# First-layer feed-forward: two of three token chunks of gate and up by one Strassen level

## The chip, the cores and the metric

One core of one Trainium2 chip. The metric is device time in microseconds (us) of one execution; a lower one is better. Engines: PE (matmuls) with its weight loads PEld, DVE (vector), ACT (scalar), POOL (GpSimd), and SP, which issues the loads from memory.

## What is computed

A decoder trunk of two layers on 1024 tokens plus 16 meta tokens, width 1024, everything float32. Each layer adds a token mixer (layer 0: pooling, layer 1: differential attention) and then a SwiGLU feed-forward with 2816 features. The change touches the feed-forward of layer 0:

```
h = h + swiglu(rms_norm(h, ffn_norm_g[i]), ffn_w_gate[i], ffn_w_up[i], ffn_w_down[i])

def swiglu(h, w_gate, w_up, w_down):
    return (jax.nn.silu(h @ w_gate) * (h @ w_up)) @ w_down
```

## The kernel before

Activations lie with the width on the partitions, as 8 tiles (k) of 128 rows. The 1040 tokens are three chunks of 348, 348 and 344 columns (`WC`). The 2816 features are 22 tiles of 128, taken in 11 pairs. Each float32 factor is split into a high part (rounded to the matmul's format by an ACT copy) and a low part (the rest, by a subtraction, mostly on DVE); `mm3` (lines 166 to 172) multiplies high x high, high x low and low x high into one PSUM bank, so that one 128 x 128 tile of a product is three matmuls.

The feed-forward of layer 0 is `ffn` (line 539). For a feature and a chunk, `phase_a` runs gate and up over 8 k-tiles into the two banks of one `psA` tile (two such tiles), then ACT takes Silu (line 556), DVE multiplies (558), ACT and DVE split the activation (561, 562). For a pair of features and a chunk, `phase_b` computes the 8 row tiles of the down product into `psB` banks (four) and DVE adds each to h (574). Gate and up weights go through a raw tile (two buffers), and high and low tiles `wh` and `wl` (four each) in `wp`; down weights are split into the eight `keep` slots `d0` to `d7`. The order inside the first pair (with mixer and norms woven in) and the last pair (with the norm of the next layer) is written out; pairs 1 to 9 (lines 618 to 625) are plain loops. `weave`, `drain` and `fill` advance several generators in turn, which gives the instructions their order; a planner that simulates a timeline then puts each engine's instructions in order by that priority, and starts what is ready when the first choice waits. All loads of weights are issued by SP, in one queue.

Layer 1's feed-forward (`wino`, line 1202, `twist_gen`, line 1128) already uses one Strassen level (Winograd's form) for its two halves of 512 tokens: a pair of features by two halves of the width is a 2 x 2 block matrix A, two halves of the width by two token halves a 2 x 2 matrix B, and seven products of half the width take the place of eight. POOL forms the sums of A's blocks (1225), `unit` splits each block (1110, 1111), the sums of B are formed once (`twist_gen`, tiles T1 to T3; T4 takes the place of a part of the input). Products 1, 6 and 5 add up in one bank X, 7 and 4 in one bank W of tile `xw`; `hold` copies a bank to SBUF by ACT (1213), `put` adds X to it by DVE (1217). So product 6 may add into X only when the put of block (0,0) has read it, product 5 only when the put of (1,0) has.

Of the kernel before, what the change touches and what calls it, by code (L numbers as in the profile page):

```python
# [8 lines left out]
F32 = mybir.dt.float32  # L9
# [90 lines left out]
class Trunk:  # L100
# [34 lines left out]
    def slot(self, i, dt, nm):  # L135
        return self.keep.tile([P, L], dt, tag=f"d{i}", name=nm)

# [149 lines left out]
    def band_setup(self, mx, raw):  # L287
        nc = self.nc
        zero = mx.tile([P, ZPAD], F32, name="zero")
        self.bt = mx.tile([P, ZPAD + 4 * (BANDW + ZPAD)], F32R, name="bt")  # L290
# [248 lines left out]
    def ffn(self, l, xn, rng, done, head=None, hook=None, tailhook=None, nf=2, pre=None, begin=None, cs=range(NCH)):  # L539
# [43 lines left out]
        def load_d(f, eng=None):  # L583
            down[f] = self.load_w(ap["down"][l * FT + f], self.keep, f"d{l}_{f}", "d", eng)

        for j, fs in enumerate(chunks):
            first, last = j == 0, j == len(chunks) - 1
            if first or last:
                if first and pre:
                    ws = {}  # L590
                else:
                    ws = {f: load_gu(f) for f in fs}
                    for f in fs:
                        load_d(f)
            if first:
# [158 lines left out]
    def scores(self, h, s, i):  # L754
# [37 lines left out]
        bias = s["bias"][:, BW - bw :]  # L792
        negm = self.sp.tile([P, 2], F32, tag="negm", name=f"negm_{h}_{i}")
        ssum = self.sp.tile([P, 2], F32, tag="ssum", name=f"ssum_{h}_{i}")
        E = []
        rs = self.sp.tile([P, 2], F32, tag="rs", name=f"rs_{h}_{i}")
        E = [None, None]
# [836 lines left out]
```

## Time and profile before

| | us |
|---|---|
| median of 3 runs | 2161.59 (2161.29 to 2165.12) |
| profiled execution | 2161.81 |
| its span, first to last instruction | 2160.0 |
| PE busy | 2101.2 (97%) |
| DVE, ACT, POOL busy | 1249.1, 809.7, 506.0 |

Busy time is the union of the intervals in which an engine had an instruction running. Matmuls overlap each other in this record, so their mean duration is longer than the time that one adds; the distance between starts is what one costs in a full stream. The granted clock is PE's, as a share of 2.4 GHz (0.50 is 1.2 GHz). The feed-forward of layer 0 runs from about 76 to 840 us, attention to about 1390, the rest is layer 1's end.

### The profile page before, as it was taken

The page shows a single profiled execution, that of the slowest core. Times are in us where ns is not written, and L with a number is a line of the kernel's source. Part 1 is how long each engine was busy: PE and PEld are TensorE (multiplying, and loading weights), DVE is VectorE, ACT ScalarE, POOL GpSimd, SP SyncE. Part 2 cuts the span into 40 slices and gives each one's busy share as a digit, 9 for nine tenths or more (in the row PEclk, how much of TensorE's full clock was granted, in tenths as well). Part 3 has the DMA queues.
Part 4 walks back from the last instruction along what each step waited for, and adds up shares of the span by engine and source line. Part 5 has one row for each costly group of instructions (what it writes and reads, how often), then busy time and mean ns, then how long its engine had stood idle before and what let it go on. Part 6 is the DMA issues. An engine that isn't in the chain of part 4 may idle for free.

```text
span 2160.0 us, 30440 instructions
## 1 busy us (share of the span) xinstructions
PE 2101.2 (97%) x12150; PEld 1952.2 (90%) x12150; DVE 1249.1 (58%) x2109; ACT 809.7 (37%) x1664; POOL 506.0 (23%) x628
## 2 busy tenths in 40 slices
PE   7999999999999999999999999998899999999997
PEld 7999999999999999999999998876788888888886
DVE  6653333433333337667667767569766666666655
ACT  5531211112111215666666665443333333333224
POOL 4300000000000015444444334137421122222113
PEclk8999999999999999999999999999999999999998
DMA  7021111111101102122111135421111111111102
GB/s 242 27 62 59 56 33 40 49 59 42 47 30 59 59 27 92 54 62 62 52 42 62 50 129 188 152 71 40 41 58 59 59 39 59 59 46 52 59 20 78
DMA packets 52696, 139.27 MB, mean 64 GB/s; under 512 B 5618, under 2 KB 17435, under 8 KB 52555
## 3 DMA queue, kind: packets, MB, share of 16 engines
q1 hardware_dynamic: 52555, 137.34, 19.5%
q8 instruction: 95, 1.56, 0.3%
q14 instruction: 46, 0.38, 0.1%
HBM read 115.16 MB, written 17.90 MB: 62 GB/s over the span
## 4 chain that ended last, share of the span: by engine, by line
PE 89%; DVE 6%; ACT 3%; DMA 1%; issue 1%; POOL 0%; SPq 0%; DVEq 0%; ACTq 0%; POOLq 0%
PE gu L171 9%; PE gu L170 8%; PE gu L172 8%; PE pj L172 4%; PE pj L170 4%; PE pj L171 4%; PE y L170 4%; PE y L171 4%; PE y L172 4%; PE yd L170 3%; PE yd L171 3%; PE yd L172 3%; PE o L860 2%; PE xw_u L170 2%; PE xw_u L172 2%; PE xw_g L171 2%
## 5 line engine op out<-in xcount | busy, mean ns | idle before, releaser
L574 DVE TENSOR_TENSOR h<-h,y 128x348 f32<-128x348 f32 (+1 forms) x264 | 134.4, 514 | 158.3 <-PE y L172 158.1
L170 PE MATMUL pj<-xh_m,w_h 128*128 128x348 f32 (+2 forms) x576 | 187.9, 326 | 0.6 <-DVE oo L896 0.6
L172 PE MATMUL pj<-xh_m,w_l 128*128 128x348 f32 (+2 forms) x576 | 185.4, 322 | 0.0
L556 ACT ACTIVATE s<-gu 128x348 f32<-128x348 f32 (+1 forms) x66 | 30.2, 458 | 412.2 <-PE gu L172 412.0
L171 PE MATMUL pj<-xl_m,w_h 128*128 128x348 f32 (+2 forms) x576 | 184.1, 320 | 0.0
L1301 DVE TENSOR_TENSOR H<-H,yd 128x512 f32<-128x512 f32 (+1 forms) x184 | 120.2, 662 | 89.1 <-PE yd L172 88.0
L199 POOL TENSOR_TENSOR acc_m<-sq_m,sq_m 128x348 f32<-128x348 f32 (+1 forms) x3 | 2.8, 929 | 673.6 <-ACT sq_m L188 673.6
L170 PE MATMUL y<-ah,d_h 128*128 128x348 f32 (+1 forms) x480 | 155.1, 324 | 3.0 <-DVE h L574 2.9
L170 PE MATMUL yd<-ah,d 128*128 128x512 f32 (+1 forms) x368 | 142.7, 392 | 12.9 <-DVE H L1301 7.8
L171 PE MATMUL y<-al,d_h 128*128 128x348 f32 (+1 forms) x480 | 154.7, 322 | 0.0
L172 PE MATMUL y<-ah,d_l 128*128 128x348 f32 (+1 forms) x480 | 154.4, 322 | 0.0
L170 PE MATMUL gu<-xh_f,g_h 128*128 128x348 f32 (+1 forms) x480 | 153.9, 321 | 0.0
L170 PE MATMUL gu<-xh_f,u_h 128*128 128x348 f32 (+1 forms) x480 | 153.9, 321 | 0.0
L171 PE MATMUL gu<-xl_f,g_h 128*128 128x348 f32 (+1 forms) x480 | 153.8, 320 | 0.0
L171 PE MATMUL gu<-xl_f,u_h 128*128 128x348 f32 (+1 forms) x480 | 153.8, 320 | 0.0
L172 PE MATMUL gu<-xh_f,g_l 128*128 128x348 f32 (+1 forms) x480 | 153.6, 320 | 0.0
L172 PE MATMUL gu<-xh_f,u_l 128*128 128x348 f32 (+1 forms) x480 | 153.5, 320 | 0.0
L171 PE MATMUL yd<-al,d 128*128 128x512 f32 (+1 forms) x368 | 142.4, 387 | 0.5 <-DVE al L1111 0.5
L172 PE MATMUL yd<-ah,d 128*128 128x512 f32 (+1 forms) x368 | 140.8, 386 | 0.0
L558 DVE TENSOR_TENSOR s<-gu,s 128x348 f32<-128x348 f32 (+1 forms) x66 | 34.1, 516 | 171.9 <-ACT s L556 171.9
L170 PEld LDWEIGHTS pj<-xh_m,w_h 128*128 128x128 f32 x576 | 108.5, 188 | 1.4 <-DVE oo L896 0.9
L171 PEld LDWEIGHTS pj<-xl_m,w_h 128*128 128x128 f32 x576 | 108.6, 188 | 0.5
(438 smaller groups left out, 5885.1 us busy)
## 6 DMA issues: line engine op xcount, KB each, us to landing
raw_d<-in_down_dram SPq DMA_DIRECT2D x42, 512.0 KB, 4.5
raw_g<-in_gate_dram SPq DMA_DIRECT2D x38, 512.0 KB, 4.5
raw_u<-in_up_dram SPq DMA_DIRECT2D x38, 512.0 KB, 4.5
raw_w<-in_wqkv_dram SPq DMA_DIRECT2D x24, 512.0 KB, 3.3
odram<-oo SPq DMA_DIRECT2D x28, 256.0 KB, 2.4
ox<-odram SPq DMA_DIRECT2D x4, 1536.0 KB, 7.1
qk<-qk SPq DMA_DIRECT2D x16, 260.0 KB, 2.9
raw_woe<-in_wo_dram SPq DMA_DIRECT2D x8, 512.0 KB, 3.6
```

Source lines behind the costliest of these rows:

```text
L170: nc.tensor.matmul(out, wh, xh, start=first, stop=False, skip_group_check=skip)
L171: nc.tensor.matmul(out, wh, xl, start=False, stop=False, skip_group_check=skip)
L172: nc.tensor.matmul(out, wl, xh, start=False, stop=last, skip_group_check=skip)
L199: eng.tensor_tensor(acc[:, :w], x[:, :w], sq[:, :w], op=ALU.add)
L556: nc.scalar.activation(st[:, :w], ps[:, 0, :w], AF.Silu)
L558: nc.vector.tensor_tensor(at[:, :w], ps[:, 1, :w], st[:, :w], op=ALU.mult)
L574: nc.vector.tensor_tensor(h[:, m, a:b], h[:, m, a:b], ps[:, :w], op=ALU.add)
L860: nc.tensor.matmul(po[:, : 2 * P], ah[:rows, kb, :], s["vhl"][:rows, kb, :], start=j == 0, stop=j == nl)
L1301: self.nc.vector.tensor_tensor(h, h, ps, op=ALU.add)
```

## The change

In layer 0, pairs 2 to 9 (eight pairs) compute gate and up of chunks 0 and 1 with the seven products; the third chunk runs beside them with the same split weight pieces as plain products (V0, V1). A side is gate or up of one pair: eight weight pieces of 512 columns (seven products, and one for the third chunk), in a ring of six tiles made of the four `wl` and the two `raw` buffers (`ring0`). The raw rows go to the four `wh` buffers (`raw0`); POOL forms the sums of blocks in place. Temporary rows come from 13 existing tiles (`t0`). The tiles T1 to T3 take all eight `keep` slots, so down weights of these pairs are split into the same ring (`down0`), and the down product of a pair is run between gate and up of the next. Pair 1 is plain, in chunk order 1, 0, 2, and the rows T are formed beside it (`twist0`, all on DVE); its down product comes with pair 2. At the end T4's part of the input is restored beside the down product of pair 9, and then the last pair loads its down weights as before. The slots grow from 1040 to 1044 columns; a zero tile of the start and three statistics tiles of attention are placed elsewhere.

```diff
         for j, fs in enumerate(chunks):
             first, last = j == 0, j == len(chunks) - 1
-            if first or last:
+            if first or last or j == 1:
                 if first and pre:
                     ws = {}
                 else:
                     ws = {f: load_gu(f) for f in fs}
-                    for f in fs:
-                        load_d(f)
...
+            elif j == 1:
+                self.nd = 0
+                tw = self.twist0(xn)
+                run = seq(*[phase_a(f, c, *ws[f]) for c in (1, 0, 2) for f in fs])
+                while not next(tw):
+                    fill(run, 3)
+                while not next(tw):
+                    fill(run, 2)
+                drain(run)
             elif last:
+                drain(self.down0(j - 1, acts), tw)
+                for f in fs:
+                    load_d(f)
...
-                for f in fs:
-                    ws = load_gu(f)
-                    load_d(f)
-                    for c in cs:
-                        drain(phase_a(f, c, *ws))
-                for c in cs:
-                    drain(phase_b(j, fs, c))
+                sg = {}
+                drain(self.gate0(j, xn, sg))
+                drain(self.down0(j - 1, acts))
+                drain(self.up0(j, xn, sg, acts))
+
+    def ring0(self, nm):
+        self.nring = getattr(self, "nring", -1) + 1
+        tag = ("wl", "raw", "wl")[self.nring % 3]
...
+    def twist0(self, xn):
...
+        for k in range(4):
+            b11, b12, b22 = part(0, 0, k), part(1, 0, k), part(1, 1, k)
+            t3 = diff(f"u3_{k}", b22, b12)
+            self.split(t3, *pair(3, k))
+            yield
+            t2 = more(f"u2_{k}", b11, t3, ALU.add)
+            self.split(t2, *pair(2, k))
+            yield
+            t1 = diff(f"u1_{k}", b12, b11)
+            self.split(t1, *pair(1, k))
+            yield
+        yield True
+        for k in range(4):
+            t4 = diff(f"u4_{k}", part(0, 1, k), [t.bitcast(F32) for t in pair(2, k)])
+            self.split(t4, *pair(4, k))
+            yield
...
+    def wino0(self, p, nm, src, xn, use):
...
+        V1 = bank("v1")[:, :w2]
+        mul(8, A[2, 1], (V1, bx(0, 2), True, False, False))
+        yield
+        V0 = bank("v0")[:, :w2]
+        mul(1, A[1, 1], (X, bx(0, 0), True, True, False), (V0, bx(0, 2), True, False, False))
+        G.tensor_tensor(A[1, 1], A[1, 1], A[2, 1], op=ALU.subtract)
+        G.tensor_tensor(A[2, 1], A[2, 1], A[2, 2], op=ALU.add)
+        yield
+        Y = bank("y0")[:, :WMAX]
+        mul(2, A[1, 2], (Y, bx(1, 0), True, True, False), (V0, bx(1, 2), False, True, False))
+        hold(0, 0, Y)
+        put(0, 0, X)
+        use(0, 2, V0)
+        yield
+        mul(7, A[1, 1], (W, bt(3), True, True, False))
+        hold(1, 1, W)
+        G.tensor_tensor(A[1, 1], A[2, 2], A[1, 1], op=ALU.subtract)
+        G.tensor_tensor(A[1, 2], A[1, 2], A[1, 1], op=ALU.subtract)
+        yield
+        mul(6, A[1, 1], (X, bt(2), False, True, True))
+        yield
+        mul(4, A[2, 2], (W, bt(4), False, True, True), (V1, bx(1, 2), False, True, False))
+        hold(1, 0, W)
+        put(1, 0, X)
+        use(1, 2, V1)
+        yield
+        Z = bank("z0")[:, :WMAX]
+        mul(3, A[1, 2], (Z, bx(1, 1), True, True, False))
+        hold(0, 1, Z)
+        yield
+        mul(5, A[2, 1], (X, bt(1), False, True, True))
+        put(0, 1, X)
+        put(1, 1, X)
+        yield
...
+    def down0(self, p, acts):
+        nc = self.nc
+        raw = [self.raw0(self.ap["down"][2 * p + i], f"raw_d0_{p}_{i}") for i in range(2)]
+        a = {(i, c): acts.pop((2 * p + i, c)) for i in range(2) for c in range(NCH)}
+        for q in range(2):
+            u = [self.unit0(raw[i][:, q * HALF : q * HALF + HALF], f"d0_{p}_{q}{i}") for i in range(2)]
+            for e in range(4):
+                m = 4 * q + e
+                for c in range(NCH):
+                    ps = self.psb(f"y0_{p}_{m}_{c}")[:, : WC[c]]
+                    for i in range(2):
+                        ww = [t[:, e * P : e * P + P] for t in u[i]]
+                        self.mm3(ps, ww, a[i, c], i == 0, i == 1)
+                    h = self.hs[c][:, m, : WC[c]]
+                    nc.vector.tensor_tensor(h, h, ps, op=ALU.add)
+                yield
```

## Rows read from the trace of the kernel before

**Rows 1.** The page: busy time of each engine with its share of the span and its instructions, PE's granted clock in 40 slices (tenths), and the chain that ended last by engine.

```profile
PE 2101.2 (97%) x12150; PEld 1952.2 (90%) x12150; DVE 1249.1 (58%) x2109; ACT 809.7 (37%) x1664; POOL 506.0 (23%) x628
...
PEclk8999999999999999999999999999999999999998
...
PE 89%; DVE 6%; ACT 3%; DMA 1%; issue 1%; POOL 0%; SPq 0%; DVEq 0%; ACTq 0%; POOLq 0%
```

**Rows 2.** Busy time by stretches of 100 us in the feed-forward of layer 0: stretch, its length, busy us and instructions of PE, PEld, DVE, ACT and POOL, granted clock, share of the load engines, GB/s.

```profile
200.00:300.00 100.00, 100.00 (x634) 100.00 (x634) 36.54 (x65) 12.58 (x20) 0.00 (x0) 1.00 0.12 38
300.00:400.00 100.00, 100.00 (x635) 100.00 (x634) 33.94 (x54) 20.34 (x31) 0.00 (x0) 1.00 0.17 52
400.00:500.00 100.00, 100.00 (x634) 100.00 (x633) 41.12 (x72) 14.58 (x24) 0.00 (x0) 1.00 0.14 44
```

**Rows 3.** Instructions of PE in order of time, first and last of 37 starts in a row (start us, us, engine, line, operation).

```profile
208.40 0.32 PE L170 MATMUL y<-ah,d_h 128*128 128x348 f32 x1
...
214.08 0.32 PE L170 MATMUL y<-ah,d_h 128*128 128x344 f32 x1
```

**Rows 4.** The page's groups of instructions: one line of `mm3` in the down product and in gate, over the ten pairs 1 to 10 (count, busy us, mean ns of one).

```profile
L170 PE MATMUL y<-ah,d_h 128*128 128x348 f32 (+1 forms) x480 | 155.1, 324 | 3.0 <-DVE h L574 2.9
...
L170 PE MATMUL gu<-xh_f,g_h 128*128 128x348 f32 (+1 forms) x480 | 153.9, 321 | 0.0
```

**Rows 5.** The same table of stretches as rows 2, in layer 1's feed-forward with its seven products.

```profile
1600.00:1700.00 100.00, 100.00 (x443) 82.84 (x442) 65.42 (x83) 34.92 (x61) 24.31 (x15) 1.00 0.16 53
1700.00:1800.00 100.00, 100.00 (x443) 82.84 (x442) 62.50 (x83) 30.25 (x52) 18.77 (x12) 1.00 0.16 53
1800.00:1900.00 100.00, 100.00 (x442) 82.80 (x442) 66.24 (x86) 34.08 (x59) 20.48 (x13) 1.00 0.16 53
```

**Rows 6.** Groups in the stretch 1600 to 2000 us, engine by engine: low halves of weight pieces of 512 columns (from a sum, z; of down), of activations, put; ACT's copies of a piece and of a bank; POOL's sums.

```profile
L1111 DVE TENSOR_TENSOR al<-cu,ah 128x512 fp32r<-128x512 f32 x28 | 41.5, 1482 | 1.0
L1111 DVE TENSOR_TENSOR d<-raw_d,d 128x512 fp32r<-128x512 f32 x27 | 29.9, 1128 | 0.0
...
L1111 DVE TENSOR_TENSOR w_g<-z,w_g 128x512 fp32r<-128x512 f32 x28 | 19.3, 689 | 23.0 <-ACT w_g L1110 23.0
...
L1217 DVE TENSOR_TENSOR cu<-cu,xw_u 128x512 f32<-128x512 f32 x28 | 18.6, 686 | 32.1 <-ACT cu L1213 27.1 <-PE xw_u L172 5.0
...
L1110 ACT CAST w_g<-z 128x512 fp32r<-128x512 f32 x28 | 17.4, 622 | 30.9 <-PE xw_u L172 19.3 <-issue 11.6
...
L1225 POOL TENSOR_TENSOR z<-raw_u 128x512 f32<-128x512 f32 x14 | 22.5, 1626 | 101.1 <-DMA raw_u<-in_up_dram 101.1
```

**Rows 7.** Groups in the stretch 160 to 800 us, each shape by itself: DVE's add to h, low half of 1024 columns, low half and multiply of 348; ACT's copy and Silu of 348.

```profile
L574 DVE TENSOR_TENSOR h<-h,y 128x348 f32<-128x348 f32 x149 | 76.0, 515 | 99.5 <-PE y L172 99.5
...
L160 DVE TENSOR_TENSOR g_l<-raw_g,g_h 128x1024 fp32r<-128x1024 f32 x18 | 22.1, 1225 | 46.2 <-ACT g_h L156 46.2
...
L562 DVE TENSOR_TENSOR al<-s,ah 128x348 fp32r<-128x348 f32 x39 | 20.3, 521 | 21.0 <-ACT ah L561 20.9
L558 DVE TENSOR_TENSOR s<-gu,s 128x348 f32<-128x348 f32 x39 | 20.3, 521 | 168.3 <-ACT s L556 168.3
...
L561 ACT CAST ah<-s 128x348 fp32r<-128x348 f32 x39 | 18.8, 483 | 22.9 <-DVE s L558 22.9
L556 ACT ACTIVATE s<-gu 128x348 f32<-128x348 f32 x39 | 18.0, 461 | 405.1 <-PE gu L172 405.1
```

**Rows 8.** Instructions in order of time around one hand-over of bank X in layer 1: the last matmul of product 4, another product's first, ACT's hold, DVE's put and what follows it, the first matmul of product 5.

```profile
1622.79 0.39 PE L172 MATMUL xw_u<-x_f,w_u 128*128 128x512 f32 x1
1623.02 0.39 PE L170 MATMUL y_g<-x_f,w_g 128*128 128x512 f32 x1
1623.22 0.58 ACT L1213 COPY cu<-xw_u 128x512 f32<-128x512 f32 x1 [2.04 <-PE xw_u L172]
...
1623.83 0.69 DVE L1217 TENSOR_TENSOR cu<-cu,xw_u 128x512 f32<-128x512 f32 x1 [1.94 <-ACT cu L1213]
...
1624.56 0.69 DVE L1283 TENSOR_TENSOR cu<-cu,cg 128x512 f32<-128x512 f32 x1
...
1625.74 0.39 PE L170 MATMUL xw_u<-T,w_u 128*128 128x512 f32 x1
```

**Rows 9.** Instructions in order of time: a low half of 512 columns on DVE beside a sum on POOL.

```profile
1673.20 1.62 POOL L1225 TENSOR_TENSOR z<-z,raw_g 128x512 f32<-128x512 f32 x1
1673.60 1.77 DVE L1111 TENSOR_TENSOR al<-cu,ah 128x512 fp32r<-128x512 f32 x1
```

**Rows 10.** Groups of PE in the stretch 120 to 154.8 us (to the end of pair 0's down product): the first and the last of the six groups of pair 1's gate and up (five of 8, one of 7).

```profile
L172 PE MATMUL gu<-xh_f,g_l 128*128 128x348 f32 x8 | 2.6, 322 | 0.0
...
L172 PE MATMUL gu<-xh_f,u_l 128*128 128x348 f32 x7 | 2.2, 320 | 0.0
```

**Rows 11.** The table of stretches in layer 1 while its rows T are formed.

```profile
1480.00:1500.00 20.00, 14.73 (x53) 10.71 (x51) 19.96 (x19) 5.43 (x11) 16.84 (x11) 0.83 0.15 52
1500.00:1520.00 20.00, 12.54 (x46) 9.60 (x47) 20.00 (x22) 4.01 (x7) 15.26 (x10) 0.91 0.00 1
1520.00:1540.00 20.00, 16.21 (x63) 12.64 (x62) 18.16 (x20) 7.22 (x13) 12.56 (x8) 0.91 0.16 53
```

**Rows 12.** The page's list of loads: count, KB each, median us from issue to landing.

```profile
raw_g<-in_gate_dram SPq DMA_DIRECT2D x38, 512.0 KB, 4.5
```

More of the change, by code (lines that the diff above doesn't have):

```diff
@@ L135, in slot @@
     def slot(self, i, dt, nm):
-        return self.keep.tile([P, L], dt, tag=f"d{i}", name=nm)
+        return self.keep.tile([P, 3 * WMAX], dt, tag=f"d{i}", name=nm)
     def small(self, dt, nm):
@@ L288, in band_setup @@
         nc = self.nc
-        zero = mx.tile([P, ZPAD], F32, name="zero")
+        zero = self.tp.tile([P, WMAX], F32, tag="xt", bufs=3, name="zero")[:, :ZPAD]
         self.bt = mx.tile([P, ZPAD + 4 * (BANDW + ZPAD)], F32R, name="bt")
@@ new lines, in wino0, with hold, put, bank @@
+    def wino0(self, p, nm, src, xn, use):
+        nc, ap = self.nc, self.ap
+        V, G = nc.vector, nc.gpsimd
+        held = {}
+        def hold(i, j, b):
+            t = held[i, j] = self.t0(f"c{nm}0_{p}_{i}{j}")
+            nc.scalar.copy(t, b)
+        def put(i, j, b):
+            t = held.pop((i, j))
+            V.tensor_tensor(t, t, b, op=ALU.add)
+            use(i, j, t)
+        raw = [self.raw0(ap[src][2 * p + i], f"raw_{nm}0_{p}_{i}") for i in range(2)]
+        A = {(i + 1, k + 1): raw[i][:, k * HALF : k * HALF + HALF] for i in range(2) for k in range(2)}
+        w2 = WC[2]
+        xw = self.psa(f"xw_{nm}0_{p}")
+        X, W = (xw[:, i, :WMAX] for i in range(2))
+        def bank(t):
+            return self.psb(f"{t}_{nm}0_{p}")
+        def mul(n, a, *jobs):
+            hi, lo = self.unit0(a, f"w{n}_{nm}0_{p}")
+            for k in range(4):
+                ww = [t[:, k * P : k * P + P] for t in (hi, lo)]
+                for out, b, first, last, skip in jobs:
+                    self.mm3(out, ww, [b(hl, k) for hl in range(2)], first and k == 0, last and k == 3, skip=skip)
+        def bx(i, j):
+            return lambda hl, k: xn[j][hl][:, 4 * i + k, : WC[j]]
+        def bt(n):
+            return lambda hl, k: self.T0[n, hl, k]
+        V1 = bank("v1")[:, :w2]
[32 more added lines that the diff above has]
+        yield
@@ new lines, in gate0, with use, up0 @@
+    def gate0(self, p, xn, s):
+        def use(i, j, t):
+            if j == 2:
+                d = self.t0(f"s2_{p}_{i}")[:, : WC[2]]
+            else:
+                d = t
+            s[i, j] = d
+            self.nc.scalar.activation(d, t, AF.Silu)
+        yield from self.wino0(p, "g", "gate", xn, use)
+    def up0(self, p, xn, s, acts):
+        nc = self.nc
+        def use(i, j, t):
+            d = s.pop((i, j)) if j == 2 else t
+            nc.vector.tensor_tensor(d, t, d if j == 2 else s.pop((i, j)), op=ALU.mult)
+            ah = self.small(F32R, f"ah0_{p}_{i}_{j}")[:, : WC[j]]
+            al = self.fp.tile([P, WMAX], F32R, tag="al", name=f"al0_{p}_{i}_{j}")[:, : WC[j]]
+            self.split(d, ah, al)
+            acts[2 * p + i, j] = (ah, al)
+        yield from self.wino0(p, "u", "up", xn, use)
@@ L792, in scores @@
         bias = s["bias"][:, BW - bw :]
[L793 to L796, printed above, removed]
+        st6 = self.sp.tile([P, 6], F32, tag="st6", name=f"st6_{h}_{i}")
+        negm, ssum, rs = (st6[:, 2 * z : 2 * z + 2] for z in range(3))
         E = [None, None]
```

46 lines of the change are left out of this document (added).

## The prediction

> **What bounds the kernel now.** I read the page first: the busy shares, the granted clock and the chain that ended last [rows 1]. TensorE (PE) is busy 97% of the span and PE lines make up 89% of the chain, so the first question is whether the stretch that the change rewrites is part of that. The table of stretches over the first layer's feed-forward says yes [rows 2]: in each 100 us from 200 us on PE is busy 100 us, at a granted clock of 1.00 (2.4 GHz), with 634 or 635 matmuls, while VectorE (DVE) is busy 34 to 41 us, ScalarE (ACT) 13 to 20 us and GpSimd (POOL) none. Nobody else is near the bound, so a matmul taken out there is worth its whole spacing, as long as what replaces it keeps PE fed.
>
> "Mean ns of one" is no price for a matmul: the groups say 321 ns, and 634 of those would be over 200 us. Matmuls overlap in the trace. The price is the distance between starts: from 208.40 to 214.08 us lie 36 matmuls of 348 columns [rows 3], 5.68 us / 36 = **157.8 ns**.
>
> **What goes.** Per pair of features and chunk, the plain form takes 2 features x 2 matrices x 8 k-tiles x 3 = 96 matmuls, so 288 for three chunks, and 8 x 2 x 3 x 3 = 144 for the down product: 432. That agrees with the counts of the groups: ten pairs give 480 per line and tile [rows 4]. With the change, one matrix of one pair takes seven products of 4 x 3 = 12 matmuls for chunks 0 and 1 (84 instead of 96, all of 348 columns), and the third chunk still takes 48. So 264 + 144 = 408 per pair, 24 fewer; over the eight pairs **192 fewer matmuls, 192 x 157.8 ns = 30.3 us**. The pairs at the two ends keep their 432.
>
> The Trainium skill, "TensorE: Matmul & The Clock Gate", section "Back-to-back issue gap", prices a matmul alone in a warm stream at N/2.4 + 2.5 ns, 147.5 ns for 348 columns; by that the same 192 would be worth 28.3 us. The rows at 157.8 ns (348) and at 100 us / 443 = 226 ns (512, [rows 5]) lie some 10 ns above it, and the rows decide.
>
> **What is added, in the steady pairs.** Per pair, from rows of the kernel before: DVE makes 20 low halves of 512 columns (8 weight pieces for each matrix, 4 for down) at 0.69 us, the price that layer 1's pieces have when POOL is quiet [rows 6]; 8 adds out of PSUM (put), 6 multiplies and 6 low halves of activations at 0.52 us; 24 adds to h at 0.515 us [rows 7]. 13.8 + 4.2 + 3.1 + 3.1 + 12.4 = 36.6 us, of 408 x 157.8 ns = 64.4 us of PE. ACT: 20 x 0.62 + 8 holds and 6 Silu at 0.46 + 6 at 0.48 = 21.7 us. POOL: 8 sums of 512 at 1.63 us = 13.0 us. Worst for DVE: every weight piece at 1.13 us and every activation step at 1.77 us, the prices beside POOL [rows 6, 9], gives 22.6 + 4.2 + 21.2 + 12.4 = 60.4 us, still under 64.4. So no engine but PE becomes the bound by sum. The nearest row for the whole is layer 1, which runs the same scheme on 512 columns: from 1600 to 1900 us PE is busy 100 of each 100 us with DVE at 63 to 66, ACT at 30 to 35 and POOL at 19 to 24 [rows 5]. The shares worked out here (57, 34, 20%) are the same or less. I take 0 us of stall for the sum.
>
> What is tighter than in layer 1 is the **hand-over of the accumulator**. Product 6 adds into the bank that the first put must have read, product 5 into the bank that the put of (1,0) must have read. In layer 1 [rows 8]: the last matmul of the earlier product starts at 1622.79 and has streamed by 1623.02, ACT's hold runs at 1623.22, DVE's put at 1623.83 and is followed at 1624.56, and the next user of the bank starts at 1625.74. That is 1.5 us of work under 2.72 us of another product. With 348 columns hold and put take 0.46 + 0.52 us and the same gaps, 1.3 us, under 12 x 157.8 ns = 1.89 us: 0.6 us is spare. A DVE step that lies in front of the put costs 0.69 us, which makes a stall of about 0.1 us; one of 1.77 us makes 1.3 + 1.77 - 1.89 = 1.2 us. There are two hand-overs on each of 16 sides. PE's order can also put down products or the third chunk between, as layer 1 does. Bounds 0 to 38 us; I take 1 us in all, nearest to layer 1's zero.
>
> PSUM banks: V0, V1, Y and Z of a side share four banks with the down product. A down result holds its bank for 6 x 157.8 ns = 0.95 us plus the add, about 0.7 us; two free banks cover that (0.83 us per result against 0.95), one does not (0.7 us of stall per result). It belongs to the same bounds.
>
> **The twist, in pair 1.** The rows T take 15 steps for each of four k, 60 DVE steps of 348 columns at 0.52 us = 31.2 us, plus 16 ACT copies (16 more DVE steps restore the input at the exit, 8.3 us under 22.7 us of down products: 0). They can write their slots 4 to 7 only when the down weights of pair 0 have been read, at about 154.8 us. By then 47 of pair 1's 288 gate and up matmuls were done [rows 10]; 241 are left, 38.0 us, and gate of pair 2 has 60 more (third chunk, products 1 and 2) that need no T, 9.5 us: 47.5 us of cover. DVE's own work in that time: 2 low halves of 1.22, 12 steps of 0.52 and 3 pieces of 0.69 us are 10.8 us; with 31.2 that is 42.0. It fits, with 5 us spare, and the 22.7 us of down products of pair 1 can go in front. I take 0. The other bound is layer 1's own twist, where DVE was busy nearly 60 of 60 us and PE got 162 matmuls in instead of 266 at 226 ns: 23 us lost, with the granted clock down to 0.83 [rows 11].
>
> **The two ends.** Pair 1 now loads both features' gate and up first, and they hold all four high and low weight tiles; gate of pair 2 draws its raw tiles from the same slots, so its second half can land only when the third segment from the end has been read, 48 matmuls = 7.6 us ahead. Landing is 4.5 us [rows 12], copy and low half 1.3 us: 5.8, so 1.8 us spare. SP issues them in turn; nothing else is queued there but such loads. I take 0.5 us, bounds 0 to 6. At the exit the last pair's four gate and up weights share those slots with the raw down weights of pair 9, and its down loads need the slots of T. PE has pair 9's 144 down products (22.7 us) as cover; if one load were late, 4.5 + 2 x 1.3 = 7 us. I take 1 us, bounds 0 to 7. The down weights that leave the keep slots move the same bytes by the same queue: 0, covered by the 20 us of the other matrix's products. In attention, the three small statistics tiles become slices of one tile with as many buffers: 0 us, bounds minus to plus 2 (the plan of later work may shift a little).
>
> **Sum.** The profiled execution took 2161.8 us (span 2160.0), the median is 2161.6: the same. 2161.8 - 30.3 + 1 + 0 + 0.5 + 1 = **2134.0 us**.
>
> **Rivals.**
> (a) Hand-overs leak: 0.3 to 0.5 us at each of the 32, 10 to 16 us: 2141 to 2148. For it: 0.6 us spare and DVE twice as busy as before. Against: no stall in layer 1 and other products to put between. Chance 0.14.
> (b) The twist stalls as in layer 1: half to all of 23 us, 2144 to 2155. For it: DVE at 42 of 47.5 us. Against: these steps take 0.52 us and POOL is quiet, there 1.7 us. Chance 0.13.
> (c) Slower. The mechanism is the same hand-over, but with a low half that shares its time with POOL in front of the put: 1.77 us instead of 0.69 beside a POOL sum of 1.62 [rows 9]. At each of 32 it costs 1.2 us: 2131.5 + 38 = 2169 us. It decides from 30.3 / 32 = 0.95 us per hand-over. Against: only 8 POOL sums per pair, and two hand-overs per side need not both meet one. Chance 0.05.
> The Trainium skill, "SBUF — State Buffer", section "SBUF: two separate sides", says the same of the port that DVE steps with two SBUF inputs share with POOL: whoever starts first holds it for the whole instruction. The trace agrees in direction; by the page's full wait a step would take 0.69 + 1.62 = 2.31 us, above the 1.77 us of the row, and (c) would come to 2187 us.
> (d) It doesn't do what it says: matmuls go but the end doesn't move, since something after them sets it (DVE or a load chain in the new form): 2161. PE at 100% speaks against it. Chance 0.03.
> (e) PE stays fed and the later plan falls better: 2126 to 2130. Chance 0.03.
>
> **How the numbers follow.** My forecast, PE fed with up to 8 us of stall (2131 to 2140), has 0.62. The range 2130 to 2150 takes in that, (a) and about half of (b): 0.62 + 0.14 + 0.06 = 0.82. A measurement here tells about 0.2% (4.3 us) from no change, so faster is below 2157.3: forecast, (a), (b) and (e), 0.92; same 0.03; slower 0.05.
>
> **What would show it.** PE's count should be 12150 - 192 = 11958; between some 230 and 750 us PE busy 100% at clock 1.00 with 634 matmuls per 100 us, DVE at 55 to 65%, POOL near 20%. Stalls of rival (a) or (c) would stand as PE waiting for DVE puts on tile xw, twice per side; those of (b) as PE waiting for T near 190 to 205 us with a lower clock. What makes the prediction wrong is any wait that repeats on all 16 sides.

## The result and the profile after

The changed kernel takes **2138.22 us**, median of 4 runs (2135.57 to 2138.96); the kernel before takes 2163.36 us on the same chip (4 runs, 2161.29 to 2165.55). The ratio is **0.9881, 95% interval 0.9864 to 0.9899**: 25 us less. The measured time is 4.2 us above the forecast of 2134.0 us and inside the stretch that the forecast gave to its likeliest case (2131 to 2140). Of these 4.2 us, 1.6 are the base: the forecast took 27.8 us off a single execution of 2161.8 us. The other 2.7 us fell short in the change itself. The four executions of each kernel lie 3.4 and 4.3 us apart, so a difference of 1 or 2 us is read from the traces, and each of those is one execution. The profiled run took 2137.84 us, its span is 2136.1 us.

The page of the changed kernel, its engines and the granted clock in 40 slices, against [rows 1]:

```profile
PE 2073.9 (97%) x11958; PEld 1923.6 (90%) x11958; DVE 1359.7 (64%) x2363; ACT 883.6 (41%) x1860; POOL 589.0 (28%) x692
...
PEclk8999999999999999999999999998999999999998
```

TensorE has 11958 matmuls, 192 fewer, and 27.3 us less busy time. The other three engines got more work (VectorE 111 us, ScalarE 74, POOL 83) and TensorE's share is still 97%.

The table of stretches over the first layer's feed-forward, against [rows 2] (stretch, length, busy us and instructions of PE, PEld, DVE, ACT, POOL, granted clock, DMA share, GB/s):

```profile
200.00:300.00 100.00, 100.00 (x633) 100.00 (x633) 51.21 (x96) 29.11 (x58) 15.54 (x12) 1.00 0.15 50
...
400.00:500.00 100.00, 100.00 (x634) 100.00 (x633) 54.24 (x101) 28.33 (x56) 15.54 (x12) 1.00 0.14 43
...
600.00:700.00 100.00, 100.00 (x634) 100.00 (x633) 54.30 (x102) 28.40 (x56) 15.51 (x12) 1.00 0.10 33
```

TensorE starts as many matmuls per 100 us as before, 633 to 635, at full clock, and the list of its waits from 130 to 690 us is empty. In the steady pairs the change costs no wait. VectorE is at 51 to 54% and POOL at 15.5%, a little under the 55 to 65 and 20 of the forecast.

The last 120 us before attention tell another story. TensorE's waits from 690 to 812 us in the changed kernel (us in total, times, longest):

```profile
PE y L170 <- DVE h L574: 2.7, 2, 2.3
PE mr_m L245 <- DVE st_m L241: 1.9, 1, 1.9
PE gu L170 <- DVE s L558: 0.9, 1, 0.9
```

and in the same stretch of the kernel before (700 to 840 us):

```profile
PE y L170 <- DVE h L574: 2.9, 2, 2.2
```

The first wait is old; two are new (a third, of 0.2 us, stands at the first projection). The wait for `s` is at the end of the last Strassen side: the last pair's gate and up wait for the multiply that frees their bank, and VectorE has restoring steps in front of it. The wait for `st_m` is for chunk 0's norm statistics. SyncE's loads show how the second came about (start, us, instruction):

```profile
709.04 0.33 SPq L144 DMA_DIRECT2D raw_g<-in_gate_dram  x1
710.94 0.33 SPq L144 DMA_DIRECT2D raw_u<-in_up_dram  x1
744.46 4.11 SPq L649 DMA_DIRECT2D raw_d<-in_down_dram  x2
```

The last pair's four gate and up weights hold all four `wh` slots, so pair 9's raw down weights are asked for only at 744.46 us. TensorE is not idle meanwhile: it does the last pair's gate and up first (to 763 us). But then both down products stand at the end, with no gate and up left to put between, and the norm sums of chunk 0 come 16 us before the first projection (795.71 against 811.71 us). Before the change they came 30.5 us ahead of it (809.14, 839.68), with gate and up between.

To place the time I use milestones of TensorE: the last `pm` (the front of the layer), the first `pj` (attention's first projection), the first gate matmul of layer 1, the last `xw_g` there (that is, almost all of its Strassen work), and the end of the final sums. Worked out from the traces, in us:

```
                        before    after   difference
start to last pm        110.73   109.11     -1.6
last pm to first pj     728.95   702.60    -26.35
pj to layer 1's gate    589.13   590.09     +1.0
gate to last xw_g       577.89   580.52     +2.6
last xw_g to the end    143.70   143.70      0.0
end                    2150.40  2126.02    -24.4
```

So the rewritten part gave 26.35 us where 30.3 us of matmuls were taken out. In this profile another 2.6 us went in layer 1, where nothing was changed; the four executions of the changed kernel alone lie 3.4 us apart, and the experiments below do not bear out that the change is the cause.

### The profile page after: what moved, and what is told of

It is laid out like the page before. It is cut to its first block, busy times and chain, and to the rows that moved or that the text cites. A ratio compares the mean times of both kernels' runs of the same rounds, so it can differ in the third digit from the quotient of the medians.

```text
span 2136.1 us, 30678 instructions
## 1 busy us (share of the span) xinstructions
PE 2073.9 (97%) x11958; PEld 1923.6 (90%) x11958; DVE 1359.7 (64%) x2363; ACT 883.6 (41%) x1860; POOL 589.0 (28%) x692
## 4 chain that ended last, share of the span: by engine, by line
PE 86%; DVE 7%; ACT 3%; DMA 2%; issue 1%; POOL 0%; SPq 0%; DVEq 0%; ACTq 0%; POOLq 0%
PE pj L170 4%; PE pj L171 4%; PE pj L172 4%; PE y L170 3%; PE y L172 3%; PE y L171 3%; PE yd L170 3%; PE yd L171 3%; PE yd L172 3%; PE xw_g L172 3%; PE xw_g L170 3%; PE xw_g L171 3%; PE gu L171 3%; PE xw_u L172 3%; PE xw_u L170 3%; PE xw_u L171 3%
## 5 line engine op out<-in xcount | busy, mean ns | idle before, releaser
L1305 ACT CAST w_u<-raw_u 128x512 fp32r<-128x512 f32 x91 | 55.0, 621 | 228.5 <-PE y L172 115.3
L170 PE MATMUL y<-ah,d 128*128 128x348 f32 (+1 forms) x432 | 138.3, 320 | 0.0
L171 PE MATMUL y<-al,d 128*128 128x348 f32 (+1 forms) x432 | 138.0, 320 | 0.0
L172 PE MATMUL y<-ah,d 128*128 128x348 f32 (+1 forms) x432 | 135.7, 320 | 0.0
L1306 DVE TENSOR_TENSOR w_g<-raw_g,w_g 128x512 fp32r<-128x512 f32 x91 | 76.1, 842 | 66.9 <-ACT w_g L1305 60.3
L172 PEld LDWEIGHTS pj<-xh_m,w_l 128*128 128x128 f32 x576 | 108.3, 188 | 0.3
L1011 ACT ACTIVATE e<-s,st 128x144 f32<-128x144 f32 (+6 forms) x112 | 78.8, 705 | 39.6 <-DVE e L1021 20.0
L170 PEld LDWEIGHTS yd<-ah,d 128*128 128x128 f32 x368 | 70.6, 193 | 26.7 <-DVE H L1496 8.2
L1306 DVE TENSOR_TENSOR d<-raw_d,d 128x512 fp32r<-128x512 f32 x80 | 68.1, 863 | 39.0 <-ACT d L1305 38.9
L1305 ACT CAST w_g<-raw_g 128x512 fp32r<-128x512 f32 x91 | 56.5, 623 | 79.6 <-PE xw_u L172 35.0
L1043 DVE TENSOR_TENSOR atl<-at,ath 116x512 fp32r<-116x512 f32 (+3 forms) x112 | 62.0, 571 | 39.5 <-ACT ath L1042 39.1
```

Source lines behind the costliest of these rows:

```text
L170: nc.tensor.matmul(out, wh, xh, start=first, stop=False, skip_group_check=skip)
L171: nc.tensor.matmul(out, wh, xl, start=False, stop=False, skip_group_check=skip)
L172: nc.tensor.matmul(out, wl, xh, start=False, stop=last, skip_group_check=skip)
L1011: nc.scalar.activation(ev, main[m], AF.Exp, bias=nm, accum_out=sm)
L1043: nc.vector.tensor_tensor(al[:rows, b0 : b0 + len(grp), :], pt[:rows, : len(grp), :], hv.bitcast(F32), op=ALU.subtract)
L1305: self.nc.scalar.copy(hi, src)
```

## The experiments

All ratios are to the kernel before on the same chip. Theory: steady pairs and twist are fully fed, the matmul term is right, and the shortfall of some 4 us is the exit (either the order of the loads there, or VectorE's work). Rivals: hand-overs leak a little everywhere; the matmul is worth less than 157.8 ns; the smaller edits cost something.

**The price of a matmul.** In the kernel before, 192 matmuls of the kind that went are left out (the low-weight product for three k-tiles, so the result is not the reference's):

```diff
-                self.mm3(ps[:, s, :w], ww, (xh[:, k, a:b], xl[:, k, a:b]), k == 0, k == KT - 1)
+                if 4 <= f < 20 and c < 2 and 0 < k < 4:
+                    nc.tensor.matmul(ps[:, s, :w], ww[0], xh[:, k, a:b], start=False, stop=False)
+                    nc.tensor.matmul(ps[:, s, :w], ww[0], xl[:, k, a:b], start=False, stop=False)
+                else:
+                    self.mm3(...)
```

> The kernel before, with the low-weight product of k-tiles 1 to 3 left out for chunks 0 and 1 in gate and up of pairs 2 to 9: the same 192 matmuls of 348 columns fewer, and nothing added or moved. It measures the price of the term by itself. My theory: 192 x 157.8 ns = 30.3 us, 2162.5 - 30.3 = 2132 (2130 to 2134). Rival 1 (the price is too high, matmuls alone are worth only the 25 us that the change brought): 2137 to 2138. Rival 2 (the page's formula for an isolated matmul): 28.3 us, 2134.

2131.50 us (2128.09 to 2134.85) against 2162.20, ratio 0.9852 (0.9827 to 0.9877): 30.7 us by the medians. The interval, 26.6 to 37.4 us, does not tell 30.3 from 28.3; the trace does. In it the way from `pm` to `pj` is 698.42 us, 30.53 less. The term of 30.3 us holds, and the changed kernel takes 702.60 - 698.42 = **4.2 us** more than this. Two kernels further down that have the same exit (the doubled twist and layer 1's twist on VectorE) took 701.46 and 702.90 us, so the price is 3.0 to 4.5 us.

Where it arises is seen by counting matmuls from the last `pm` in both traces: the changed kernel is 0.5 us behind after 3800 of them (at 710 us), 1.9 us after 4000 (743 us), 1.7 us after 4200 (775 us) and 4.2 us at the first projection. So entry, twist and all steady pairs together cost 0.5 us, the last side 1.4 and the stretch of the norm at the end 2.3.

**The edits beside the Strassen level alone**, in the kernel before: the longer slots, the zero tile's place, the three statistics in one tile.

```diff
-        return self.keep.tile([P, L], dt, tag=f"d{i}", name=nm)
+        return self.keep.tile([P, 3 * WMAX], dt, tag=f"d{i}", name=nm)
...
-        zero = mx.tile([P, ZPAD], F32, name="zero")
+        zero = self.tp.tile([P, WMAX], F32, tag="xt", bufs=3, name="zero")[:, :ZPAD]
...
+        st6 = self.sp.tile([P, 6], F32, tag="st6", name=f"st6_{h}_{i}")
+        negm, ssum, rs = (st6[:, 2 * z : 2 * z + 2] for z in range(3))
```

> The kernel before with the side edits alone: slots of 1044 columns, the zero tile from the temporary pool, three statistics tiles of attention as slices of one. My theory: no difference, ratio 0.999 to 1.001. Rival (the slices tie steps of attention together and cost what fell short): 2 to 6 us slower, ratio 1.001 to 1.003.

2163.14 us, ratio 1.0001 (0.9990 to 1.0012). They cost nothing.

**How much the hand-overs can bear.** Three more VectorE steps of 0.52 us ahead of each of the two puts that free a bank, on all 16 sides:

```diff
+            if (i, j) in ((0, 0), (1, 0)):
+                for _ in range(3):
+                    V.tensor_tensor(t, t, t, op=ALU.max)
```

> The changed kernel with three more DVE steps of 348 columns, 0.52 us each, in front of the two puts (0,0) and (1,0) of each side, whose bank the next product waits for. By my prediction's reckoning (one product of 1.89 us as the only cover, 1.3 us of work): 1.3 + 1.56 - 1.89 = 1.0 us of stall at 32 hand-overs, 31 us: as slow as before, 2169. By what the trace of the changed kernel shows (4.1 us of other products between product 4 and product 5): no stall in the steady pairs, PE at 634 matmuls per 100 us, 2138 to 2141, at most a stall at the last side.

2141.70 us (2 runs), ratio 0.9901 (0.9878 to 0.9924): 3.5 us above the changed kernel, with overlapping intervals, where the forecast's reckoning gave 31 us. The list of TensorE's waits from 130 to 700 us stays empty; the one that grows stands on the last side:

```profile
PE gu L170 <- DVE s L558: 2.5, 1, 2.5
```

2.5 instead of 0.9 us is the dose of 3 x 0.52 us, once; from `pm` to `pj` the kernel takes 704.08 us, 1.5 more. The other 2 us I could not tie to the edit (the front of the profiled run, where nothing was edited, ended at 113.12 us, 4.0 later than in the changed kernel and the latest of all). Why the steady hand-overs have room is seen in the changed kernel without the added steps, instructions in order of time (start, us):

```profile
323.59 0.32 PE L172 MATMUL xw_u<-xh_f,w_u 128*128 128x348 f32 x1
...
323.95 0.45 ACT L718 COPY cu<-xw_u 128x348 f32<-128x348 f32 x1 [1.22 <-PE xw_u L172]
...
324.43 0.52 DVE L722 TENSOR_TENSOR cu<-cu,xw_u 128x348 f32<-128x348 f32 x1 [0.98 <-ACT cu L718]
...
324.95 0.69 DVE L1306 TENSOR_TENSOR w_g<-raw_g,w_g 128x512 fp32r<-128x512 f32 x1
...
328.00 0.32 PE L170 MATMUL xw_u<-tw,w_u 128*128 128x348 f32 x1
```

Hold and put are over at 324.95 us, the next user of the bank starts at 328.00: 3.05 us to spare, because TensorE's order puts products of the next pair's gate (`xw_g`, `v_g`, `y_g`) between. This is [rows 8] with the same chain but a longer cover.

**The twist, doubled.** The sums for T formed twice, 44 more VectorE steps or 22.9 us:

```diff
-            V.tensor_tensor(d, a[0], b[0], op=op)
-            V.tensor_tensor(e, a[1], b[1], op=op)
-            V.tensor_tensor(d, d, e, op=ALU.add)
+            for _ in range(2 if nm[1] in "1234" else 1):
+                V.tensor_tensor(d, a[0], b[0], op=op)
+                V.tensor_tensor(e, a[1], b[1], op=op)
+                V.tensor_tensor(d, d, e, op=ALU.add)
...
-            V.tensor_tensor(d, a[0], b, op=op)
-            V.tensor_tensor(d, d, a[1], op=ALU.add)
+            for _ in range(2):
+                V.tensor_tensor(d, a[0], b, op=op)
+                V.tensor_tensor(d, d, a[1], op=ALU.add)
```

> The changed kernel with the sums for the rows T1 to T4 formed twice (44 more DVE steps of 0.52 us, 22.9 us, in pair 1). My theory: 42 us of DVE lay under 47.5 us of gate and up and 22.7 us of down products, 5 us spare before the first product that needs T and more with the down products; so 2138 to 2148, the stall at 190 to 215 us. Rival (DVE time in pair 1 is the bound as in layer 1): the whole 22.9 us, 2161.

2138.28 us (2 runs), ratio 0.9885 (0.9862 to 0.9908): the same as the changed kernel. Even with VectorE full, TensorE misses nothing in the table of stretches:

```profile
160.00:180.00 20.00, 20.00 (x127) 19.99 (x127) 20.00 (x48) 3.67 (x8) 0.00 (x0) 1.00 0.01 1
180.00:200.00 20.00, 20.00 (x129) 20.00 (x128) 18.86 (x34) 7.70 (x17) 5.86 (x4) 1.00 0.32 107
```

**The exit, by the order of loads.** The last pair's gate and up are loaded behind pair 9's down weights:

```diff
-            if first or last or j == 1:
+            if first or j == 1:
...
                 drain(self.down0(j - 1, acts), tw)
+                ws = {f: load_gu(f) for f in fs}
```

> The changed kernel, but the last pair's four gate and up loads are issued behind the down product of pair 9 and no longer in front of it. My theory: some 4 us of the 6 that the change fell short were lost at the exit, because the last pair's weights held all four wh tiles, pair 9's down product ran only after the last pair's gate and up, and the norm of chunk 0 had no work left beside it. Then this kernel is 2 to 4 us faster than the changed one (2138.2): 2134 to 2136, ratio to the kernel before 0.987, and pair 9's raw down weights are issued before 715 us. Rival (the loss is in the steady pairs or in later stages): no difference, 2137 to 2139.

2138.06 us, ratio 0.9884 (0.9862 to 0.9906): a miss, nothing gained. The wait for `st_m` is gone, but others came, 690 to 815 us:

```profile
PE y L170 <- DVE h L574: 2.9, 2, 2.3
PE y L170 <- ACT ah L1306: 2.1, 1, 2.1
PE xw_u L170 <- DVE cu L723: 1.1, 1, 1.1
PE y L171 <- DVE al L1307: 0.8, 1, 0.8
```

Without the last pair's products to put between, the last side runs back to back, its hand-over shows (`xw_u` for `cu`), and the down product waits for activations that are queued behind the restoring steps. From `pm` to `pj` it takes 705.40 us, 2.8 more than the changed kernel. In this profile layer 1 took 2.8 us less (577.77), so its end is the same; the times do not tell the two kernels apart.

**The exit, half and half.** Only the first feature of the last pair is loaded ahead:

```diff
-                    ws = {f: load_gu(f) for f in fs}
+                    ws = {f: load_gu(f) for f in (fs[:1] if last else fs)}
...
+                ws[fs[1]] = load_gu(fs[1])
```

> The changed kernel, but of the last pair only the first feature's gate and up are loaded in front of pair 9's down product, the second feature's behind it. My theory after the run of the exit order: at the exit PE needs other products beside the last side (its hand-overs and its last activations stand behind the restoring steps on DVE), and the end needs gate and up of chunk 2 left as cover for chunk 0's norm. The changed kernel has the first and not the second (4 us lost up to the first projection), the exit order the second and not the first (7 us). This has both: 3 to 4 us faster than the changed kernel, 2134 to 2136 us, with under 1 us of PE idle between 700 and 760. Rival (whatever the order, DVE's 8 us of restoring steps end up on the path): 2138 or more, PE idle of 2 us or more there.

2137.79 us, ratio 0.9884 (0.9869 to 0.9899): a miss again; `pm` to `pj` 703.63 us, 1.0 more than the changed kernel. The wait for `st_m` is gone here too. The waits from 690 to 815 us:

```profile
PE y L170 <- DVE h L574: 3.8, 2, 2.3
PE y L170 <- ACT ah L1306: 3.1, 1, 3.1
```

**The exit without restoring**, on top of that split (the last pair's chunk 1 is then worked out from other data):

```diff
-            b12 = diff(f"ub_{k}", part(0, 0, k), [t.bitcast(F32) for t in pair(1, k)], ALU.add)
-            self.split(b12, *pair(4, k))
```

> The kernel with the split exit, with the 20 steps that put the input of chunk 1's lower half back before the last pair left out: that half stays the sum T4, so the last pair's chunk 1 is worked out from other data than the reference's. Theory (the exit is bound by VectorE, whose restoring steps stand ahead of the activations that the down products wait for): 20 steps of some 0.55 us leave VectorE's queue in the stretch from 705 to 730 us, TensorE's waits for the steps h and ah there shrink from some 9 us in all to under 5, and the time is 2133 to 2135.5 us. Rival (the exit is bound by the loads and the slots, or by something in layer 1): the waits move to another releaser and the time stays at 2137 to 2138.5 us.

2135.71 us (2135.47 to 2136.17), ratio 0.9878 (0.9864 to 0.9893), 2.1 us under the split exit by the medians, with overlapping intervals; `pm` to `pj` 701.73 us, 1.9 less, and TensorE's waits come to 4.9 us instead of 6.9. (Of the 20 steps 16 are VectorE's, 8.3 us, and 4 are copies on ScalarE; the expectation put them all on VectorE.) Some 2 us of the exit are the restoring steps. The number is just above the range that the theory gave, and a wait remains:

```profile
PE y L170 <- DVE h L574: 3.0, 2, 2.2
PE y L170 <- ACT ah L1304: 1.9, 1, 1.9
```

**Restoring shared with POOL**, 8 of the 16 steps, also on top of the split:

```diff
+        def diff(nm, a, b, op=ALU.subtract, eng=V):
...
-            V.tensor_tensor(e, a[1], b[1], op=op)
+            eng.tensor_tensor(e, a[1], b[1], op=op)
...
+            b12 = diff(f"ub_{k}", part(0, 0, k), [...], ALU.add, self.nc.gpsimd)
+            self.split(b12, *pair(4, k), self.nc.gpsimd)
```

> The kernel with the split exit, with 8 of the 20 restoring steps (the second sum of each k-tile and its low half) on GpSimd in place of VectorE. Theory (VectorE bounds the exit): 8 x 0.55 = 4.4 us leave VectorE, of which 1 to 3 us show in the time: 2135 to 2137 us. Rival (the steps on GpSimd slow those of VectorE beside them, as the rows of layer 1 show): the same time or up to 2 us more than with the split exit, 2137.5 to 2140 us.

2138.68 us, ratio 0.9891 (0.9876 to 0.9906); `pm` to `pj` 703.78 us, the same as the split exit. The rival's time came. From 710 to 720 us VectorE is as busy with 15 steps as it was with 20 (first row this kernel, second the split exit):

```profile
710.00:720.00 10.00, 8.78 (x54) 8.19 (x52) 9.28 (x15) 5.48 (x12) 5.28 (x5) 1.00 0.01 2
```
```profile
710.00:720.00 10.00, 9.05 (x56) 8.57 (x55) 9.29 (x20) 5.63 (x12) 0.16 (x1) 1.00 0.04 16
```

The restoring `ub_1d` took 1.26 us there, and the low halves of down pieces 1.00 us on average instead of 0.69: what went to POOL came back as longer steps.

**Strassen in pairs 2 to 5 only**, pairs 6 to 9 plain, so that the exit lies where nothing of the norm or attention is near:

```diff
             elif last:
-                drain(self.down0(j - 1, acts), tw)
...
+            elif j > 5:
+                if j == 6:
+                    drain(self.down0(j - 1, acts), tw)
+                ws = {f: load_gu(f) for f in fs}
+                for f in fs:
+                    for c in cs:
+                        drain(phase_a(f, c, *ws[f]))
+                drain(self.down0(j, acts))
```

> The changed kernel with the seven products in pairs 2 to 5 only; pairs 6 to 9 run gate and up plain, with their down weights in the ring, and the input is restored beside the down product of pair 5. My theory: each pair is worth its full 3.8 us and the ends cost nothing when the loads are in good order: 4 x 3.8 = 15 us faster than before, 2147 (2145 to 2149). Rival (each steady pair hides a loss of 0.6 to 0.8 us): 12 us faster or less, 2150 or more; PE would show waits in the steady pairs.

2159.73 us, ratio 0.9986 (0.9973 to 0.9999), far from the expected half of the gain. From `pm` to `pj` 724.28 us: 4.67 less than before where 96 matmuls, 15.1 us, went. Some 9 of the missing 10.5 us stand in one place, the exit:

```profile
440.00:450.00 10.00, 9.93 (x63) 9.65 (x62) 7.65 (x15) 4.66 (x10) 0.34 (x2) 1.00 0.00 1
450.00:460.00 10.00, 4.64 (x22) 3.54 (x21) 9.21 (x21) 4.54 (x10) 0.00 (x0) 0.92 0.14 52
460.00:470.00 10.00, 10.00 (x50) 10.00 (x49) 3.93 (x9) 1.05 (x1) 0.00 (x0) 0.73 0.18 54
```

VectorE is full from 450 to 460 us with 21 steps while TensorE works 4.64 of 10 us, and after the pause TensorE is granted 0.73 of its clock (a mean over 10 us in which it stood at either of its levels, 1.2 and 2.4 GHz) and gets 50 matmuls in instead of 65. TensorE's waits there are for a hand-over (`cu`, 1.9 us), for the high half of the next gate weights (`g_h`, 1.8) and for an activation (`al`, 1.6). So moving the exit away from the norm did not make it cheaper: some 9 us here, 3.7 in the changed kernel. That the order leaves nothing to put between is the likely reason; it is not shown by itself, since the edit also loads pair 6's gate and up behind the down product.

**Layer 1's twist on VectorE alone.** This tests the other place where time went missing. In `twist_gen`:

```diff
-        V, G = nc.vector, nc.gpsimd
+        V = G = nc.vector
```

> The changed kernel with layer 1's rows T formed by DVE alone, as layer 0's are, and no longer by DVE and POOL. It asks why layer 1's twist lost some 20 us of PE time and layer 0's none. My theory: the sharing with POOL makes DVE's steps 1.2 to 1.8 us where they take 0.69 alone, so moving POOL's 28 or so steps to DVE costs less than it frees: steps at 0.69 us, 5 to 12 us faster than the changed kernel (2126 to 2133). Rival (the sum of the work is what counts): DVE gets some 25 steps more and this is 5 us or more slower, 2143 or more.

2133.46 us (2132.84 to 2136.93), ratio **0.9862 (0.9846 to 0.9878)**, 4.8 us under the changed kernel by the medians and the fastest here that computes all of the reference. Its interval overlaps the changed kernel's (0.9864 to 0.9899); the next experiment makes the gain certain. Groups of VectorE from 1450 to 1510 us, first in the changed kernel, then with the edit (count, busy us, mean ns of one, idle before):

```profile
L1306 DVE TENSOR_TENSOR d<-raw_d,d 128x512 fp32r<-128x512 f32 x3 | 5.3, 1767 | 0.0
L1306 DVE TENSOR_TENSOR w_g<-z,w_g 128x512 fp32r<-128x512 f32 x4 | 4.5, 1115 | 0.0
L1332 DVE TENSOR_TENSOR t_2d<-x_f,x_f 128x512 f32<-128x512 f32 x2 | 3.5, 1786 | 0.0
```
```profile
L1306 DVE TENSOR_TENSOR w_g<-z,w_g 128x512 fp32r<-128x512 f32 x4 | 2.7, 682 | 0.0
...
L1306 DVE TENSOR_TENSOR d<-raw_d,d 128x512 fp32r<-128x512 f32 x3 | 2.1, 688 | 1.0 <-ACT d L1305 0.9
...
L1332 DVE TENSOR_TENSOR t_2d<-x_f,x_f 128x512 f32<-128x512 f32 x2 | 1.4, 686 | 0.0
```

Beside POOL's share of the twist, steps of 0.69 us take 1.1 to 1.8; taking the helper away is faster. How the two engines meet is seen in the changed kernel (start, us):

```profile
1481.79 1.71 POOL L1420 TENSOR_TENSOR z<-raw_u 128x512 f32<-128x512 f32 x1
1482.30 0.67 DVE L1496 TENSOR_TENSOR H<-H,yd 128x512 f32<-128x512 f32 x1
1482.89 1.15 DVE L1340 TENSOR_TENSOR t_2d<-t_2d,x_f 128x512 f32<-128x512 f32 x1
...
1610.29 1.62 POOL L1420 TENSOR_TENSOR z<-z,raw_u 128x512 f32<-128x512 f32 x1
1610.68 1.77 DVE L1306 TENSOR_TENSOR al<-cu,ah 128x512 fp32r<-128x512 f32 x1
```

The steps `t_2d` and `al` start 1.10 and 0.39 us after a sum of POOL and both end 0.55 us after that sum has ended (1483.50 and 1611.91 us); the step `H`, which reads a PSUM bank (`yd`), takes its 0.67 us in the middle of the sum. From the gate to the last `xw_g` of layer 1, 91 of VectorE's 128x512 steps that read SBUF alone start during a step of POOL. All but one of them end 0.54 to 0.56 us after it, whatever part of it they met (the other started 0.07 us before POOL's end and took 0.68 us). It holds the other way too: 12 of POOL's 128x512 steps that start while VectorE runs none take 1.29 to 1.32 us, and 89 that start during a VectorE step reading SBUF alone end 1.12 to 1.19 us after that step. So each waits until the other is done.

In the profiles less of the gain shows than in the times. The profiled execution is the slowest of its four and ends 1.6 us before the changed kernel's. From the gate to the first product of up it takes 97.48 us against 108.96, to the last `xw_g` 577.24 against 580.52.

**The same edit in the kernel before**, to see whether it mends what the change lost in layer 1:

> The kernel before, with layer 1's twist steps all on VectorE (the edit that made the changed kernel some 4.8 us faster). In layer 1 the profiled run of the kernel before takes 107.2 us from the first gate matmul to the first product of up, that of the changed kernel 108.95 with the same order of TensorE, and the changed kernel with this edit 97.5. Theory (the 2.6 us that the changed kernel loses in layer 1 are the phase of the granted clock behind the twist's stalls, which this edit shortens away): before has less to gain here, 1.5 to 3 us, so 2159 to 2160.5 us against 2162, and the change is worth 27 us or more between the two edited kernels. Rival (the edit is worth the same 4.8 us in either kernel, and the 2.6 us have another cause): 2157 to 2158 us, the change worth 25 us.

2156.88 us (11 runs, 2155.56 to 2162.50), ratio 0.9972 (0.9964 to 0.9981): 5.5 us, and clear of no change. That the edit would gain less here than in the changed kernel falls: it pays for itself, in either. From gate to the last `xw_g` this kernel took 574.86 us, the two edited ones with the change 577.24 and 576.71 (one profile each), so the edit does not remove a difference of that size.

**Split exit, shared restoring and layer 1's twist together:**

> The split exit, the restoring steps shared with GpSimd, and layer 1's twist steps all on VectorE, in one kernel. If the two places are independent, the 4.8 us that the second edit gave alone and the 0 to 3 us of the first add up: 2130 to 2133.5 us. Rival (what is gained at the exit is lost again in the phase of the granted clock in layer 1): 2133 to 2136 us.

2135.66 us (2135.04 to 2137.52), ratio 0.9881 (0.9864 to 0.9897). The time misses the expected sum of the two gains. The exit edits add nothing (`pm` to `pj` 704.16 us); the kernel is no faster than layer 1's edit alone, whose interval it overlaps. The best version is the changed kernel with the twist of layer 1 on VectorE.

## Why the prediction was nearly right

- **The bound.** Right: TensorE is full in the stretch, and removing its work there moves the end; rival (d) falls.
- **192 x 157.8 ns = 30.3 us.** Right; leaving out 192 matmuls gave 30.5 us in the trace. The Trainium skill, "TensorE: Matmul & The Clock Gate", section "Back-to-back issue gap", has a formula for a matmul alone, from which 28.3 us was estimated; the trace does not agree, and the spacing in [rows 3] was the better price.
- **No engine but TensorE becomes the bound.** Right. POOL's sums took 1.29 us, not the 1.63 of layer 1 (which has a wait for VectorE in it), so the sum was on the safe side.
- **Hand-overs, 1 us taken of 0 to 38.** They cost no wait. The step that failed is the spare of 0.6 us: it counted one product as the only cover, though the text said that others can stand between. The cover was 4.4 us between starts (323.59 to 328.00) and the spare 3.05 us. That three added steps vanish everywhere but on the last side, where nothing else is left, shows it. With it rival (a) falls, and (c) too, whose price of 1.2 us at each of 32 needed that spare. Long steps did occur: seven of gate's low halves between 200 and 690 us started during a sum of POOL and took 1.24 to 1.80 us, and TensorE did not wait.
- **The price in (c).** The Trainium skill, "SBUF — State Buffer", section "SBUF: two separate sides", says that whichever of VectorE and POOL starts first holds the shared port for its whole instruction. The traces bear that out in size too, not only in direction: the 90 steps above end a fixed 0.55 us after POOL. The prediction misread its row. By the rule a step waits for what is left of POOL's instruction, and in [rows 9] the sum had started 0.40 us earlier, so 1.22 us were left, and 1.22 + 0.55 = 1.77 us is what the step took. Even a start together would give 1.62 + 0.55 = 2.17 us, not 2.31.
- **Twist, 0 us.** Right, with more room than 5 us: another 22.9 us of VectorE work went in free. Rival (b) falls.
- **Entry, 0.5 us of 0 to 6.** No wait from 130 to 690 us. Entry, twist and hand-overs together made 0.5 us.
- **Exit, 1 us of 0 to 7.** This is the term that was mis-sized: 3.7 us of the 4.2. The prediction looked at loads that might land late under 22.7 us of pair 9's down products. The loads do come late (744.46 us), but the cover was not pair 9's down products, which wait for them; it was the last pair's gate and up, used up early, so that chunk 0's norm statistics stood bare (1.9 us of wait). And the 8.3 us of restoring steps, taken at 0 "under 22.7 us of down products", stand in VectorE's queue ahead of the last pair's multiply (0.9 us of wait) and, with the split exit, ahead of activations that the down products need (worth 2 us there). Moving the loads only trades one wait for the other. The two new waits make 2.8 of the 3.7 us; the remaining 0.9 us I could not tie to one wait.
- **After the exit.** The forecast let everything behind attention's start shift as it is. In the profile 1.0 us went in attention and 2.6 us in layer 1. The first is within what this part scatters (588.7 to 593.1 us over all kernels here). The second can't be put down to the change. TensorE's order there is the same in both kernels. Of the other kernels without an edit there, seven took 577.4 to 577.9 us from gate to the last `xw_g`, six of them with the change (one of these in four pairs only); one with the change took 579.1, and the kernel before with 192 matmuls left out took 580.2. What goes along with it is the granted clock from the gate to the first product of up: 0.87 in the two longest, 0.89 in the one of 579.1, 0.90 to 0.95 in the seven and in the kernel before. Whether the lower clock is the cause and what sets it off is open, and no kernel was profiled twice to see how far one kernel's executions differ there. The changed kernel and the kernel before in that stretch:

```profile
1401.80:1510.76 108.96, 91.09 (x362) 72.54 (x361) 95.75 (x102) 42.88 (x70) 67.48 (x43) 0.87 0.12 39
```
```profile
1428.81:1535.97 107.16, 86.92 (x361) 68.65 (x360) 99.38 (x102) 43.00 (x70) 67.72 (x43) 0.94 0.12 40
```

Taken together: 30.3 - 4.2 leaves 26.1 us, and the trace has 26.35 between `pm` and `pj`, where the forecast had 27.8. It came that close partly by luck: the exit cost 2.7 us more than was taken for it, and entry and hand-overs 1.0 us less. The front of this run was 1.6 us shorter, the later parts 3.6 us longer: 24.4 us at the end of the trace, 25 by the medians.

## What to carry to other kernels

Matmuls taken out of a stretch in which TensorE is full are worth their spacing in the trace, and side work is free while there are independent products to put between; so cost the last round, where there are none, by itself: list what each engine's queue holds there and which wait the next stage ends on. A slot shared by two kinds of load also fixes the order of the work behind them, not only when a load lands. And an engine that helps can slow the one it helps: compare the durations of the same step with and without it before sharing work, and compare when the two engines' steps end, which tells a wait from a slower step.

## What was not expected of the hardware

- VectorE and POOL waited for each other step by step where both read SBUF alone: 90 of 91 VectorE steps of 128x512 that started during a step of POOL in layer 1 ended 0.54 to 0.56 us after it, so that they took 0.84 to 1.82 us against 0.69. Steps that add a PSUM bank kept their 0.67 to 0.69 us. With half of layer 1's twist on POOL, the whole kernel took 4.8 to 5.5 us more by the medians. At the exit, 8 steps moved to POOL left VectorE 9.28 us busy of 10 with 15 steps in place of 20.
- POOL's sum of two tiles of 128x512 took 1.29 us in the changed first layer, where [rows 6] have 1.63 us. The longer ones in layer 1 are those that started during a VectorE step.
- The same order of TensorE in layer 1 took 577.4 to 580.5 us in different kernels, the longest with the lowest granted clock (0.87) up to the first product of up.
